# Summing the last gathered tile's value rows on VectorE, and taking the last dense column tile by tile, in a one-core encoder layer

## The chip, the cores and the metric

The kernel runs on one core of a Trainium2 chip. The time is device time in microseconds (us) of one launch. A core has TensorE (PE, with its weight loads as PEld), VectorE (DVE), ScalarE (ACT), GpSimd (POOL) and SyncE (SP), each with an instruction queue of its own that it works off in order, and 16 DMA engines that serve all queues.

## The reference

One encoder layer on 1024 tokens of width 1024: a projection, two token mixers, a merge, a layer norm, and then a layer of product-key experts (PEER) and a second layer norm. The change touches only the experts and the last norm:

```python
def _peer(x, w_q, sub_keys, u_table, v_table):
...
        q = (xb @ w_q).reshape(t, PEER_HEADS, 2, PEER_HALF)
...
        idx = jnp.take_along_axis(cand_i.reshape(t, PEER_HEADS, K * K), best_pos, axis=-1)
        gate = jax.nn.softmax(best_s, axis=-1).astype(xb.dtype)
        h = jax.nn.gelu(jnp.einsum('thkd,td->thk', u_table[idx], xb), approximate=False)
        return jnp.einsum('thk,thkd->td', gate * h, v_table[idx])
...
        x = _layer_norm(DN_ALPHA * x + _peer(x, peer_w_q[l], peer_sub_keys[l], peer_u[l], peer_v[l]),
                        ln2_g[l], ln2_b[l])
```

For each token 8 heads x 16 = 128 experts are selected out of 16384. Each expert has one key row in `u_table` and one value row in `v_table`, 1024 float32 each. The token's output is the sum over its 128 slots of gate x gelu(key row . x) x value row.

## The kernel before, in words

The 1024 tokens are 8 tiles of 128. Tiles 3, 4, 5 (`DENSE`) are computed densely, over all 16384 experts, on TensorE. Tiles 0, 1, 2, 6, 7 (`GATHERED`) gather only the rows that they selected.

**The dense loop.** `dense_block` runs over 128 columns j of 128 experts each. `hidden(j, m)` multiplies the key rows of a column with the hidden states of all three tiles into the PSUM tile `b` (24 products in two halves m). `csplit(j)` applies gelu on ScalarE, multiplies with the gates on VectorE (tile `C`), and splits the result into a high and a low part (`ch`, `cl`). `values(j, m)` multiplies that with one half of the column's value rows (`vh`, `vl`) into the six accumulators `po` (tiles `v`, 18 products a column). All products are done as three products of split operands; `usplit` and `vsplit` make these from the raw rows `uraw` and `vraw`: a cast on ScalarE and a subtraction on VectorE for one half and on GpSimd for the other. The raw rows, 512 KB for keys and 512 KB for values a column, are loaded through SP's queue, two and three columns ahead. Stage and place of everything else are told by the column.

**The gathered tiles.** For each slot k, `experts_in` has GpSimd issue an indirect DMA that fetches the key row of each of the 128 tokens (L1461, 512 KB, into the places `g` or `C` of `keys`), and VectorE reduces it against x into one column of `hh` (L1467). When a tile's 128 slots are done, `hh` goes through gelu and the gate and is stored to `cijd`. Then `Rows` takes over: `prepare` loads it and turns it on TensorE; `gather` has GpSimd issue indirect DMAs for value rows (L1763, 512 KB, into `vr` or `C`), where token and slot are arranged such that TensorE sums them with narrow products into the PSUM tile `pg`: 4 products for a pair of rows, each shown as 2 instructions in the trace, 16 for the two pairs that are done in one go. The sum is stored to `yd`, and `finals` loads it again, adds alpha x, normalizes and stores the tile.

**What sets the order.** PE, DVE and POOL issue in the order in which the code is written. `Background` objects put the gathered work between the products: each product of t us gives `rate` x t us of credit to `g.V` (`Rows`, rate `RATEV`) and to `g.B` (`experts_in`, rate `RATEB`), and a step with a cost is taken while there is credit. In the dense loop the rates before were 0.46 for `g.B` and 0.52 for `g.V`, and 1.25 for `g.V` once all keys were done. So tile 7's values came after its keys: its keys ended at column 103, and its value products filled columns 105 to 125.

**The end.** `finals` is stepped twice a column from column 44. For tile 7 and then for the dense tiles the norm ran after the loop on VectorE (`add` L1829, statistics L1266, `scale` L1277 and L1278).

Of the kernel before, what the change touches and what calls it, by code (L numbers as in the profile page):

```python
# [10 lines left out]
F32 = mybir.dt.float32  # L11
# [4 lines left out]
AF = mybir.ActivationFunctionType  # L16
OP = mybir.AluOpType
# [9 lines left out]
TKI = 1  # L27
RATEP = (1, 1, 0.9)

RATEB = (2.1, 0.46)  # L30
RATEV = (4.2, 0.52, 1.25)
SEL = (1, 2, 3)
DENSE = (3, 4, 5)
GATHERED = (0, 1, 2, 6, 7)
LATE = (4, 5, 6)

RING = 7
# [24 lines left out]
ALPHA = 2.0 ** 0.25  # L62
# [232 lines left out]
class Weights:  # L295
# [965 lines left out]
def layer_norm(g, mt, z):  # L1261

    dve, act = g.dve, g.act
    st = mt.tile([128, 2, 6], F32, name="st", bufs=3)
    for i in range(2):
        dve.bn_stats(st[:, i, :], z[:, i * 512:(i + 1) * 512])  # L1266
    yield
    mv = mt.tile([128, 2], F32, name="mv", bufs=3)
    dve.bn_aggr(mv, st)
    rs = mt.tile([128, 1], F32, name="rs", bufs=3)  # L1270
    act.activation(rs, mv[:, 1:2], AF.Sqrt, bias=g.eps[:, 1:2])
    yield
    dve.reciprocal(rs, rs)
    yield

    def scale(z, gb):
        dve.scalar_tensor_tensor(z, z, mv[:, 0:1], gb[0], op0=OP.subtract, op1=OP.mult)  # L1277
        dve.scalar_tensor_tensor(z, z, rs, gb[1], op0=OP.mult, op1=OP.add)  # L1278

    yield scale  # L1280
# [166 lines left out]
def experts_in(g, tile_):  # L1447

    dve, act, pool, sp, A, P = g.dve, g.act, g.pool, g.sp, g.A, g.gp
    idx = P.tile([128, 128], I32, name="eidx", bufs=1)  # L1450
    sp.dma_start(idx, g.seld[tile_])
    xt = P.tile([128, D], F32, name="ext")
    sp.dma_start(xt, g.x1d[tile_])
    hh = P.tile([128, 128], F32, name="hh", bufs=1)
    keys, n = g.keys, 0
    yield 1.0
    yield 1.0
    for k in range(128):
        while n < 128 and len(keys.free) > 1:
            keys.alive[n] = place = keys.take()  # L1460
            pool.indirect_dma_start(out=place, out_offset=None, in_=A["u"], in_offset=bass.IndirectOffsetOnAxis(ap=idx[:, n:n + 1], axis=0))  # L1461
            n += 1
# [4 lines left out]
        dve.tensor_tensor_reduce(out=gg, in0=gg, in1=xt, scale=1.0, scalar=0.0, op0=OP.mult, op1=OP.add, accum_out=hh[:, k:k + 1])  # L1467
# [12 lines left out]
def parts(C, i, a, b):  # L1480
# [4 lines left out]
def dense_block(g, C):  # L1485


    tc, nc, A, ident = g.tc, g.nc, g.A, g.ident
    dve, act, pool, sp, pe = g.dve, g.act, g.pool, g.sp, g.pe
    tiles = DENSE  # L1490
    nt = len(tiles)
    n = nt * 128
# [62 lines left out]
    with tc.tile_pool(name="bp", bufs=BLEAD + 1) as bp, tc.tile_pool(name="cj", bufs=2) as cj:  # L1555
        ab, pb = {}, {}
        for k in range(-BLEAD - 4, n4 + 1):
# [35 lines left out]
    u_hl, v_hl, c_hl, phs = {}, {}, {}, {}  # L1593
    po = [[g.psV.tile([128, 512], F32, name=f"v{i}{m}") for m in range(2)] for i in range(nt)]
# [92 lines left out]
    fin, old = iter(()), [p for j in range(LOOP, HALF - 7, 8) for i in range(nt) for p in parts(C, i, j, j + 8)]  # L1687
    g.rows.pairs = True
    for j in range(128):
        hidden(j + 1, 0)  # L1690
        usplit(2 * j + 4)
        hidden(j + 1, 1)
        usplit(2 * j + 5)
        csplit(j + 1)
        values(j, 0)
        vsplit(2 * j + 2)
        next(fin, None)
        values(j, 1)
# [118 lines left out]
def finals(g, tiles, po, places):  # L1817


    A, dve, act, sp = g.A, g.dve, g.act, g.sp  # L1820
    gb = places[0:2]
    for m in range(2):
        sp.dma_start(gb[m], A["ln"][2 + m:3 + m, :].to_broadcast([128, D]))
    zd = places[4:7]

    def add(z, y):
        for m in range(2):
            zm = z[:, m * 512:(m + 1) * 512]
            dve.scalar_tensor_tensor(zm, zm, ALPHA, y[m], op0=OP.mult, op1=OP.add)  # L1829

    z, y = places[2:4]
    for t in GATHERED:
        sp.dma_start(z, g.x1d[t])
        if t == GATHERED[-1]:
            while f"g{t}" not in g.B.done:
                yield
            for t_, z_ in zip(tiles, zd):
                sp.dma_start(z_, g.x1d[t_])
# [86 lines left out]
```

## Time and profile before

| | us |
|---|---|
| median of 3 runs | 3575.67 (3569.68 to 3590.42) |
| the profiled execution, its own time | 3567.98 |
| its span, first to last instruction | 3566.2 |
| dense loop, from the first product into `b` to the last product into `v` | 2195.0 to 3543.7 |

| engine | busy us | share of the span |
|---|---|---|
| PE | 3168.3 | 89% |
| DVE | 2252.5 | 63% |
| POOL | 2051.0 | 58% |
| ACT | 1161.9 | 33% |

The shares are means over stages with different limits. The dense loop is the last 38% of the span and is read by itself below. In the views, a group row ends with busy time, the mean of one instruction in ns, and the idle time of the engine just before instructions of the group with what ended it; a row of the table of stretches gives busy time per engine, the granted clock of TensorE, the busy share of the DMA engines and GB/s.

### The profile page before, as it was taken

The numbers are of one execution on the slowest core, as the hardware profiler recorded it, in microseconds if no ns is written. First come the engines' busy times: TensorE is split into PE (matmuls) and PEld (weight loads), VectorE is DVE, ScalarE is ACT, GpSimd is POOL, SyncE is SP. The second block draws the span as 40 slices with busy tenths as digits, with TensorE's granted clock in tenths as the row PEclk, the third lists the DMA queues.
The fourth block names the chain that finished last, engine by engine and source line by source line (L and its number), as shares of the span: only waits on it lengthen the run. The fifth ranks groups of instructions, "written<-read, shape, count | busy, mean of one in ns | idle before, by whom it ended". The sixth has DMA issues, their size and how long they took to land. (4 is left out here: it accounts for less than half of the span.)

```text
span 3566.2 us, 55635 instructions
## 1 busy us (share of the span) xinstructions
PE 3168.3 (89%) x20656; PEld 2312.2 (65%) x20656; DVE 2252.5 (63%) x5115; ACT 1161.9 (33%) x2448; POOL 2051.0 (58%) x1682
## 2 busy tenths in 40 slices
PE   7899999999997887889677677999999999999997
PEld 5577777875565665567433323877777777776665
DVE  3244423358887997886589755777666767773324
ACT  3443222323431121101244433334333333333332
POOL 2032115315555565653365566888887788886773
PEclk9999999999998788899778899999999999999998
DMA  8373357878897788999799999999999999999994
GB/s 282 112 255 110 105 190 250 306 272 313 287 348 290 272 302 307 350 358 383 278 392 351 354 361 379 369 353 362 386 398 368 394 394 399 397 396 341 389 390 188
DMA packets 369809, 1134.72 MB, mean 318 GB/s; under 512 B 49792, under 2 KB 88448, under 8 KB 367744
## 3 DMA queue, kind: packets, MB, share of 16 engines
q0 software_dynamic: 184320, 671.17, 49.5%
q1 hardware_dynamic: 168496, 430.82, 33.3%
q10 hardware_dynamic: 16720, 29.17, 2.2%
q8 instruction: 162, 2.65, 0.3%
q14 instruction: 111, 0.91, 0.1%
HBM read 997.25 MB, written 133.76 MB: 317 GB/s over the span
## 5 line engine op out<-in xcount | busy, mean ns | idle before, releaser
L1461 POOL DMA_INDIRECT g<-u,eidx x566 | 688.9, 1217 | 520.6 <-DVE hh L1467 193.9
L1467 DVE CUSTOM_DVE_ANT_0 g<-g,ext 128x1024 f32<-128x1024 f32 x566 | 727.9, 1296 | 84.2 <-DMA g<-u,eidx 78.2
L1763 POOL DMA_INDIRECT vr<-v,ve x434 | 454.9, 1048 | 212.0 <-issue 107.2
L292 POOL TENSOR_TENSOR wl<-wraw,wh 128x1024 fp32r<-128x1024 f32 x63 | 152.9, 2427 | 434.3 <-ACT wh L291 335.2
L274 PE MATMUL pg<-vr,win 128*32 128x512 f32 x1736 | 312.9, 643 | 65.6 <-DMA vr<-v,ve 57.9
L274 PE MATMUL b<-xh,uh 128*128 128x384 f32 x1024 | 349.8, 342 | 14.0 <-DVE C L1648 12.6
L274 PE MATMUL b<-xh,ul 128*128 128x384 f32 x1024 | 351.0, 343 | 6.2 <-POOL ul L292 4.3
L274 PE MATMUL b<-xl,uh 128*128 128x384 f32 x1024 | 348.7, 341 | 0.0
L274 PE MATMUL v<-vl,ch 128*128 128x512 f32 x768 | 305.0, 397 | 11.5 <-POOL vl L292 11.4
L274 PE MATMUL v<-vh,ch 128*128 128x512 f32 x768 | 302.5, 394 | 0.0
L274 PE MATMUL v<-vh,cl 128*128 128x512 f32 x768 | 300.8, 392 | 0.0
L274 PE MATMUL pj<-xh,wh 128*128 128x512 f32 x624 | 286.0, 458 | 13.6 <-ACT xh L291 6.6
L291 ACT CAST uh<-uraw 128x512 fp32r<-128x512 f32 x256 | 158.3, 620 | 362.6 <-PE b L274 254.7
L274 PE MATMUL pj<-xl,wh 128*128 128x512 f32 x624 | 260.0, 417 | 2.7 <-DVE xl L292 2.4
L274 PE MATMUL pj<-xh,wl 128*128 128x512 f32 x624 | 259.0, 415 | 0.2 <-issue 0.2
L1763 POOL DMA_INDIRECT C<-v,ve x206 | 212.0, 1029 | 81.4 <-issue 49.0
L292 DVE TENSOR_TENSOR vl<-vraw,vh 128x512 fp32r<-128x512 f32 x128 | 140.8, 1100 | 173.9 <-ACT vh L291 113.0
L291 ACT CAST vh<-vraw 128x512 fp32r<-128x512 f32 x256 | 158.3, 620 | 244.1 <-PE v L274 183.9
L274 PEld LDWEIGHTS v<-ab 128*128 128x128 f32 x768 | 112.5, 217 | 175.6 <-issue 112.9
L292 POOL TENSOR_TENSOR ul<-uraw,uh 128x512 fp32r<-128x512 f32 x128 | 171.6, 1340 | 89.2 <-ACT uh L291 73.6
L274 PEld LDWEIGHTS b<-xh,uh 128*128 128x128 f32 x1024 | 193.5, 189 | 34.5 <-DVE C L1648 14.8
L274 PEld LDWEIGHTS b<-xh,ul 128*128 128x128 f32 x1024 | 193.5, 189 | 32.8 <-issue 24.7
(360 smaller groups left out, 6603.9 us busy)
## 6 DMA issues: line engine op xcount, KB each, us to landing
uraw<-ut SPq DMA_DIRECT2D x128, 512.0 KB
vraw<-vt SPq DMA_DIRECT2D x128, 512.0 KB
wraw<-w SPq DMA_DIRECT2D x72, 512.0 KB
wh<-whd SPq DMA_DIRECT2D x72, 512.0 KB
wl<-whd SPq DMA_DIRECT2D x72, 512.0 KB
whd<-wh SPq DMA_DIRECT2D x71, 512.0 KB
whd<-wl SPq DMA_DIRECT2D x71, 512.0 KB
cd<-S SPq DMA_DIRECT2D x12, 1344.0 KB
```

The costliest lines, as they stand in the source:

```text
L274: g.pe.matmul(o, l, r, start=start, stop=stop_)
L291: g.act.copy(hi, src)
L292: (lo_eng or g.dve).tensor_sub(lo, src, hi.bitcast(F32))
L1461: pool.indirect_dma_start(out=place, out_offset=None, in_=A["u"], in_offset=bass.IndirectOffsetOnAxis(ap=idx[:, n:n + 1], axis=0))
L1467: dve.tensor_tensor_reduce(out=gg, in0=gg, in1=xt, scale=1.0, scalar=0.0, op0=OP.mult, op1=OP.add, accum_out=hh[:, k:k + 1])
L1763: g.pool.indirect_dma_start(out=place, out_offset=None, in_=g.A["v"], in_offset=bass.IndirectOffsetOnAxis(ap=self.meta[i][1][:, t:t + 1], ...
```

## The change

- `GATHERED` loses tile 7 (`LAST`), so `Rows` has four tiles instead of five. `experts_in` of tile 7 goes on after its 128 key rows with its 128 value rows: the same index column and the same ring of places, an indirect DMA on GpSimd for each, and one `scalar_tensor_tensor` of 128x1024 on VectorE that adds value row x `hh` to a tile `z`, which starts as alpha x. The gathering runs over the border between keys and values without a stop (`ahead`). The turning, the narrow products, and the store and load of `cijd` and `yd` are gone for tile 7.
- The rates in the dense loop become 0.58 for `g.B`, 0.6 from the point where tile 7's keys are selected, and 0.45 for `g.V` throughout.
- The last column's values products are issued tile by tile (both halves of tile 3's accumulators, then tile 4's, then tile 5's) instead of half by half.
- Tile 7's norm is made within the loop. The norms of the dense tiles are made tile by tile; the scaling of the second one goes to ScalarE (x rs - mean x rs) and GpSimd (times the gain, plus the bias), with its store on ScalarE's queue.

The diff, without the lines that only rename:

```diff
-RATEB = (2.1, 0.46)
-RATEV = (4.2, 0.52, 1.25)
+RATEB = (2.1, 0.58, 0.6)
+RATEV = (4.2, 0.45)
-GATHERED = (0, 1, 2, 6, 7)
+GATHERED = (0, 1, 2, 6)
+LAST = 7
...
+    ends = 256 if tile_ == LAST else 128
+    def ahead():
+        nonlocal n
+        while n < ends and len(keys.free) > 1:
+            keys.alive[n] = place = keys.take()
+            pool.indirect_dma_start(out=place, out_offset=None, in_=A["uv"[n // 128]], in_offset=bass.IndirectOffsetOnAxis(ap=idx[:, n % 128:n % 128 + 1], axis=0))
+            n += 1
...
+    g.last = z = g.rows.places.take()
+    sp.dma_start(z, g.x1d[tile_])
+    ahead()
+    yield 3.0
+    yield 3.0
     dve.tensor_mul(hh, hh, gate)
+    dve.tensor_scalar(z, z, ALPHA, None, op0=OP.mult)
+    for k in range(128):
+        ahead()
+        gg = keys.alive.pop(128 + k)
+        dve.scalar_tensor_tensor(z, gg, hh[:, k:k + 1], z, op0=OP.mult, op1=OP.add)
+        keys.give(gg)
+        yield 1.46
...
     def values(j, m):
         ch, cl = c_hl[j]
-        vh, vl = v_hl.pop(2 * j + m)
+        if j == 127 and m == 0:
+            return
         for i in range(nt):
             s = slice(i * 128, (i + 1) * 128)
-            mm3(g, po[i][m], ch[:, s], cl[:, s], vh, vl, j == 0, j == 127)
+            for q in (m,) if j < 127 else range(2):
+                mm3(g, po[i][q], ch[:, s], cl[:, s], *v_hl[2 * j + q], j == 0, j == 127)
+        v_hl.pop(2 * j + m)
...
-        if f"g{GATHERED[-1]}" in g.B.done:
-            g.V.rate = RATEV[2]
+        if f"v{GATHERED[-1]}" in g.V.done:
+            next(fin, None)
+            next(fin, None)
+        if f"k{LAST}" in g.B.done:
+            g.B.rate = RATEB[2]
...
+    ln = layer_norm(g, g.pp, g.last)
+    for _ in range(3):
+        next(ln)
+        yield
+    next(ln)(g.last, gb)
+    sp.dma_start(A["out"][LAST * 128:(LAST + 1) * 128, :], g.last)
     while not g.over:
         yield
     lns = []
     for i, z in enumerate(zd):
         add(z, po[i])
         lns.append(layer_norm(g, g.pp, z))
-    for _ in range(3):
-        for ln in lns:
-            next(ln)
-    for t, z, ln in zip(tiles, zd, lns):
-        next(ln)(z, gb)
-        sp.dma_start(A["out"][t * 128:(t + 1) * 128, :], z)
+        next(lns[i])
+        next(lns[i])
+        if i == 1:
+            next(lns[0])
+            next(lns[1])
+            mv, rs = next(lns[1]).__defaults__
+            dve.scalar_tensor_tensor(mv[:, 0:1], mv[:, 0:1], -1.0, rs, op0=OP.mult, op1=OP.mult)
+            act.activation(z, z, AF.Identity, scale=rs, bias=mv[:, 0:1])
+            g.pool.tensor_mul(z, z, gb[0])
+            g.pool.tensor_add(z, z, gb[1])
+            act.dma_start(A["out"][tiles[1] * 128:tiles[1] * 128 + 128, :], z)
+    next(lns[2])
+    for i in (0, 2):
+        next(lns[i])(zd[i], gb)
+        sp.dma_start(A["out"][tiles[i] * 128:(tiles[i] + 1) * 128, :], zd[i])
```

How the order of instructions changes, at three places.

GpSimd's queue around column 95 of the dense loop. Before: `u,eidx` are key rows for VectorE, `v,ve` value rows for TensorE, `ul` and `vl` the subtractions of the dense splits.

```order
L292 TENSOR_TENSOR vl<-vraw,vh 128x512
L1461 DMA C<-u,eidx 128x1024
L292 TENSOR_TENSOR ul<-uraw,uh 128x512
L1461 DMA C<-u,eidx 128x1024
L1763 DMA vr_14133<-v,ve 128x1024
L1763 DMA C<-v,ve 128x1024
L1763 DMA vr_14134<-v,ve 128x1024
L1763 DMA C<-v,ve 128x1024
L292 TENSOR_TENSOR vl<-vraw,vh 128x512
L1461 DMA g_70<-u,eidx 128x1024
L1461 DMA g_71<-u,eidx 128x1024
```

The same queue near the same column in the changed kernel, where `v,eidx` are tile 7's value rows for VectorE:

```order
L293 TENSOR_TENSOR vl<-vraw,vh 128x512
L1465 DMA g_72<-v,eidx 128x1024
L1465 DMA C<-v,eidx 128x1024
L293 TENSOR_TENSOR ul<-uraw,uh 128x512
L1465 DMA C<-v,eidx 128x1024
L293 TENSOR_TENSOR vl<-vraw,vh 128x512
L1465 DMA C<-v,eidx 128x1024
L1465 DMA g_68<-v,eidx 128x1024
L1793 DMA C<-v,ve 128x1024 x3
L1793 DMA vr_14134<-v,ve 128x1024
```

Between two subtractions there stand about as many gathers as before, but more of them are for VectorE. Counted over columns 26 to 122: before 179 for VectorE and 328 for TensorE, after 295 (167 key rows, 128 value rows) and 224; over columns 3 to 25: before 45 and 60, after 57 and 54.

VectorE's queue at the same place, one column, before (`ISA` with `ext` is the key row's reduction, `hh 128x1` its result's read):

```order
L1648 TENSOR_TENSOR C<-b,C 128x3x4x32
L292 TENSOR_TENSOR cl<-C,ch 128x384
L1467 ISA g_69,hh<-g_69,ext 128x1024
L1467 ISA hh 128x1
L292 TENSOR_TENSOR vl<-vraw,vh 128x512
L1467 ISA C,hh<-C,ext 128x1024
L1467 ISA hh 128x1
L292 TENSOR_TENSOR ul<-uraw,uh 128x512
```

and after:

```order
L1672 TENSOR_TENSOR C<-b,C 128x3x4x32
L293 TENSOR_TENSOR cl<-C,ch 128x384
L1499 SCALAR_TENSOR_TENSOR C<-g_71,hh,C 128x1024
L1499 SCALAR_TENSOR_TENSOR C<-g_72,hh,C 128x1024
L293 TENSOR_TENSOR vl<-vraw,vh 128x512
L293 TENSOR_TENSOR ul<-uraw,uh 128x512
L1499 SCALAR_TENSOR_TENSOR C<-C,hh 128x1024
```

The reductions of key rows end at column 80 instead of 103, and the value sums stand from column 82 to 122, three or four in a column.

VectorE's last instructions, before: first the six additions of the dense accumulators (`v_17411` to `v_17416` are the two halves of tile 3's, tile 4's and tile 5's), then all statistics.

```order
L1829 SCALAR_TENSOR_TENSOR C<-C,v_17411 128x512
L1829 SCALAR_TENSOR_TENSOR C<-C,v_17412 128x512
L1829 SCALAR_TENSOR_TENSOR C<-C,v_17413 128x512
L1829 SCALAR_TENSOR_TENSOR C<-C,v_17414 128x512
L1829 SCALAR_TENSOR_TENSOR C<-C,v_17415 128x512
L1829 SCALAR_TENSOR_TENSOR C<-C,v_17416 128x512
L1266 BN_STATS st<-C 128x6 x6
L1269 BN_AGGR mv<-st 128x2 x3
```

and after, where the first tile's statistics stand ahead of the second tile's additions:

```order
L1859 SCALAR_TENSOR_TENSOR C<-C,v_17411 128x512
L1859 SCALAR_TENSOR_TENSOR C<-C,v_17412 128x512
L1267 BN_STATS st<-C 128x6 x2
L1270 BN_AGGR mv<-st 128x2
L1859 SCALAR_TENSOR_TENSOR C<-C,v_17413 128x512
L1859 SCALAR_TENSOR_TENSOR C<-C,v_17414 128x512
L1267 BN_STATS st<-C 128x6 x2
L1270 BN_AGGR mv<-st 128x2
L1274 RECIPROCAL rs<-rs 128x1 x2
L1903 SCALAR_TENSOR_TENSOR mv<-mv,rs 128x1
L1859 SCALAR_TENSOR_TENSOR C<-C,v_17415 128x512
```

Tile 7's statistics and scaling, which stood ahead of the first fence's rows, have gone into the loop's last columns.

More of the change, by code (lines that the diff above doesn't have):

```diff
@@ L1274, in layer_norm, with scale @@
     yield
-    def scale(z, gb):
+    def scale(z, gb, mv=mv, rs=rs):
         dve.scalar_tensor_tensor(z, z, mv[:, 0:1], gb[0], op0=OP.subtract, op1=OP.mult)
@@ L1457, in experts_in @@
     yield 1.0
+    ends = 256 if tile_ == LAST else 128
[5 more added lines that the diff above has]
+            n += 1
     for k in range(128):
[L1459 to L1462, printed above, removed]
+        ahead()
         if k == 0:
@@ L1471, in experts_in @@
         sp.dma_start(g.dbg["hh"][tile_ * 128:(tile_ + 1) * 128, :], hh)
-    gate = idx.bitcast(F32)
+    gate = g.tk.tile([128, 128], F32, name="t1") if tile_ == LAST else idx.bitcast(F32)
     sp.dma_start(gate, g.gated[tile_])
     act.activation(hh, hh, AF.Gelu)
-    dve.tensor_mul(hh, hh, gate)
-    act.dma_start(g.cijd[tile_][:, 0, :], hh)
-    yield 0.1
+    if tile_ != LAST:
+        dve.tensor_mul(hh, hh, gate)
+        act.dma_start(g.cijd[tile_][:, 0, :], hh)
+        yield 0.1
+        return
+    while not g.rows.places.room(1):
+        yield 1.0
+    g.last = z = g.rows.places.take()
[3 more added lines that the diff above has]
+    yield 3.0
+    dve.tensor_mul(hh, hh, gate)
+    dve.tensor_scalar(z, z, ALPHA, None, op0=OP.mult)
+    for k in range(128):
+        ahead()
+        gg = keys.alive.pop(128 + k)
+        dve.scalar_tensor_tensor(z, gg, hh[:, k:k + 1], z, op0=OP.mult, op1=OP.add)
+        keys.give(gg)
+        yield 1.46
 def parts(C, i, a, b):
@@ L1667, in values @@
         ch, cl = c_hl[j]
-        vh, vl = v_hl.pop(2 * j + m)
+        if j == 127 and m == 0:
+            return
         for i in range(nt):
             s = slice(i * 128, (i + 1) * 128)
-            mm3(g, po[i][m], ch[:, s], cl[:, s], vh, vl, j == 0, j == 127)
+            for q in (m,) if j < 127 else range(2):
+                mm3(g, po[i][q], ch[:, s], cl[:, s], *v_hl[2 * j + q], j == 0, j == 127)
+        v_hl.pop(2 * j + m)
         if m:
@@ L1711, in dense_block @@
             fin = finals(g, tiles, po, old[-4:] + old[0:nt])
-    assert f"v{GATHERED[-1]}" in g.V.done
+    assert f"v{GATHERED[-1]}" in g.V.done and f"g{LAST}" in g.B.done
     g.over = True
@@ L1833, in finals @@
         sp.dma_start(z, g.x1d[t])
[L1834 to L1838, printed above, removed]
         while f"v{t}" not in g.V.done:
@@ L1855, in finals @@
         yield
+    while f"g{LAST}" not in g.B.done:
+        yield
+    for t, z in zip(tiles, zd):
+        sp.dma_start(z, g.x1d[t])
+    ln = layer_norm(g, g.pp, g.last)
+    for _ in range(3):
+        next(ln)
+        yield
+    next(ln)(g.last, gb)
+    sp.dma_start(A["out"][LAST * 128:(LAST + 1) * 128, :], g.last)
     while not g.over:
```

## The prediction

> **What bounds the kernel now.** I read the page first, for the shares of the whole span, then stretches of the dense loop, then the chain that ended last, then the groups of the stretch that the change touches, and last GpSimd's and VectorE's own rows.
>
> ```profile
> span 3566.2 us, 55635 instructions
> PE 3168.3 (89%) x20656; PEld 2312.2 (65%) x20656; DVE 2252.5 (63%) x5115; ACT 1161.9 (33%) x2448; POOL 2051.0 (58%) x1682
> ```
>
> By the page PE leads and GpSimd has 42% to spare. That mean hides the stage in question:
>
> ```profile
> core 0: us, PE busy (x) PEld busy (x) DVE busy (x) ACT busy (x) POOL busy (x), PEclk, DMA share, GB/s
> 2195.00:2462.00 267.00, 257.71 (x1364) 203.93 (x1365) 185.34 (x354) 98.11 (x198) 211.96 (x172) 0.98 0.96 358
> 2462.00:3490.00 1028.00, 997.17 (x5395) 767.75 (x5394) 608.63 (x802) 370.95 (x773) 828.22 (x705) 0.99 1.01 386
> 3490.00:3544.00 54.00, 53.68 (x291) 41.97 (x289) 16.23 (x27) 19.13 (x36) 20.95 (x19) 1.00 0.48 173
> 3544.00:3566.00 22.00, 0.00 (x0) 0.00 (x0) 17.82 (x27) 0.67 (x3) 0.00 (x0) 0.55 0.24 96
> ```
>
> These are columns 0 to 25, 26 to 122, 123 to 127, and the end. In the long stretch PE is busy 97%, the DMA engines 1.01 (their packets overlap, so they are full) and GpSimd 81% without its issue gaps. Three resources are near their limits at once. The chain tells how PE's columns are made up:
>
> ```profile
> 3073.86 4.24 PE b L274 x24
> 3078.11 4.17 PE v L274 x18
> ...
> 3083.33 1.85 PE pg L274 x16
> ...
> 3088.51 4.12 PE v L274 x18
> ```
>
> A column is 4.24 + 4.12 = 8.36 us of dense products. Two pairs of gathered value rows cost 1.85 us, one pair 0.925. Now the groups of the long stretch:
>
> ```profile
> L1763 POOL DMA_INDIRECT vr<-v,ve x197 | 204.6, 1039 | 55.6 <-issue 49.8 <-DMA g<-u,eidx 0.9 <-PE pg L274 0.9
> L1763 POOL DMA_INDIRECT C<-v,ve x137 | 143.5, 1048 | 39.7 <-issue 33.5 <-DVE ve L1751 2.2 <-PE b L274 0.9
> L1461 POOL DMA_INDIRECT g<-u,eidx x110 | 136.2, 1238 | 24.3 <-issue 16.7 <-DVE hh L1467 2.4 <-DVE cl L292 1.2
> L292 POOL TENSOR_TENSOR vl<-vraw,vh 128x512 fp32r<-128x512 f32 x97 | 133.7, 1378 | 13.2 <-ACT vh L291 12.0
> L292 POOL TENSOR_TENSOR ul<-uraw,uh 128x512 fp32r<-128x512 f32 x97 | 127.9, 1318 | 49.4 <-ACT uh L291 38.1 <-issue 9.8
> L274 PE MATMUL pg<-vr,win 128*32 128x512 f32 x776 | 126.4, 602 | 0.5 <-DMA vr<-v,ve 0.5
> L274 PE MATMUL pg<-C,win 128*32 128x512 f32 x536 | 95.7, 615 | 7.2 <-DMA C<-v,ve 7.2
> L1461 POOL DMA_INDIRECT C<-u,eidx x67 | 84.0, 1254 | 17.8 <-issue 10.7 <-DMA eidx<-seld 2.8 <-DVE hh L1467 1.5
> L1648 DVE TENSOR_TENSOR C<-b,C 128x384 f32<-128x384 f32 x97 | 53.8, 555 | 113.1 <-ACT b L1647 97.0 <-ACT uh L291 10.1 <-issue 5.8
> ```
>
> L1648 stands once in a column, so these are 97 columns. PE: 97 x 8.36 = 811, and (776 + 536) / 8 = 164 pairs x 0.925 = 152, together 963 of 1028 us; 65 us are stalls. GpSimd's price of a gather is its duration with the issue gap ahead of it, which no other work fills: for VectorE (136.2 + 24.3 + 84.0 + 17.8 - 2.8) / 177 = 1.47 us, for TensorE (204.6 + 55.6 + 143.5 + 39.7) / 334 = 1.33. The two subtractions cost 133.7 + 127.9 us, with gaps that aren't waits 2.73 a column. Sum 260 + 443 + 265 = 968, that is 94% of the stretch. So GpSimd isn't the idle engine that the page shows, but one of three that are full.
>
> **Why gathers for VectorE are dearer.**
>
> ```profile
> 3111.81 1.42 POOL L292 TENSOR_TENSOR vl<-vraw,vh 128x512 fp32r<-128x512 f32 x1
> 3113.38 1.76 POOL L1461 DMA_INDIRECT g<-u,eidx  x1
> 3115.45 0.94 POOL L1763 DMA_INDIRECT vr<-v,ve  x1 [0.30 <-issue]
> 3116.69 0.94 POOL L1763 DMA_INDIRECT C<-v,ve  x1 [0.30 <-issue]
> ...
> 3120.41 1.81 POOL L1461 DMA_INDIRECT C<-u,eidx  x1 [0.31 <-issue]
> ...
> 3112.02 2.29 DVE L1467 CUSTOM_DVE_ANT_0 C<-C,ext 128x1024 f32<-128x1024 f32 x1
> ```
>
> An unhindered gather takes 0.94 + 0.30 = 1.24 us. The one at 3113.38 ends at 3115.14, 0.83 after VectorE's reduction (3114.31) lets go; that reduction itself takes 2.29 because GpSimd's subtraction (to 3113.23) held it up. The two engines lock each other out for part of an instruction. [...]
>
> **The change, part by part.**
>
> *Columns 0 to 25: 0.* Over columns 3 to 25 the key gathers go from 45 to 57 and TensorE's from 60 to 54: PE gives back 3 pairs, 2.8 us, GpSimd gets 12 x 1.47 - 6 x 1.33 = 9.7 us more, and it was busy 212 of 267 there, before gaps. I take 0, bounds -3 and +10.
>
> *Columns 26 to 122: -15.* PE loses 164 - 112 = 52 pairs, 48 us. If PE alone were the limit the stretch would shrink by that and by stalls, to between 915 and 980. But bytes and gathers stay: they only move from one consumer to the other. GpSimd: 295 x 1.47 + 224 x 1.33 + 97 x 2.73 = 434 + 298 + 265 = 997 us. At the price of the densest part of the stretch,
>
> ```profile
> L1461 POOL DMA_INDIRECT g<-u,eidx x55 | 73.7, 1340 | 11.9 <-issue 6.8 <-DVE hh L1467 1.5 <-DVE cl L292 1.2
> L1461 POOL DMA_INDIRECT C<-u,eidx x35 | 44.5, 1270 | 7.6 <-issue 5.3 <-DVE hh L1467 1.2 <-DVE cl L292 0.3
> ...
> 2854.00:3262.00 408.00, 403.19 (x2173) 320.79 (x2172) 281.18 (x359) 148.30 (x302) 342.34 (x281) 1.00 1.02 393
> ```
>
> (137.7 / 90 = 1.53), it is 1014. DMA: 1028 us x 386 GB/s = 397 MB now; 519 gathers instead of 511 in the trace make it 401 MB; at the 393 GB/s of the densest part, with its share of 1.02, that takes 1020 us. Two independent limits thus stand at 997 to 1020 where PE needs 915. I take 1013, near the upper ones, because GpSimd was never without some idle time: 1028 to 1013 is -15. The bounds are 980 (below) and 1056 (rival A). The same engines then show another picture: PE idle some 10%, waiting for `ul` and `vl` behind gathers in GpSimd's queue. The stall at the passage from tile 7's keys to its values goes (the 7.2 us of the row `pg<-C,win`, part of the 65). VectorE gets 116 more rows of about 1.4 us in this stretch, 162 us on 609 of 1028, so 75%; its splits and `C` come later behind a sum of 1.2 us, which PE's next products cover (L1648 is wanted after the 4.12 us of `v`). Where this cover goes, PE stalls by the rest of the sum, at most 1.2 us a column. SP's queue has the same row loads; the store and load of `yd` for tile 7 and the turning of its `cijd` are gone, which costs nothing now at a DMA share of 0.48 in the last columns. ScalarE loses the small copies for 64 pairs; it is busy 36% and gates nothing.
>
> *Columns 123 to 127: -5.* Before, 8 pairs of tile 7 stand there, after 2 of tile 6: -5.5 us. In the last column taking tile 4's and 5's products later means that the second half of tile 3 needs the last split after 0.69 us instead of 2.06, while that split takes 1.3 us (0.63 on ScalarE, 0.69 on VectorE, rows below): +0.7. Tile 7's norm and two switches of ScalarE's function stand here too; they lie beside 4.24 us of `b`, and I take 0, at worst +2.
>
> *The end: -5.*
>
> ```profile
> 3539.50 0.63 ACT vh L291
> 3540.15 0.69 DVE vl L292
> 3540.85 1.20 DVE C L1829 x2
> ...
> 3546.52 3.59 DVE C L1829 x6
> 3550.11 3.57 DVE st L1266 x6
> ...
> 3560.93 1.28 DVE C L1278
> ...
> L292 POOL TENSOR_TENSOR wl<-wraw,wh 128x1024 fp32r<-128x1024 f32 x63 | 152.9, 2427 | 434.3 <-ACT wh L291 335.2 <-PE s L274 42.7 <-PE po L274 26.4
> ```
>
> Before, tile 7's norm holds VectorE until 3546.52, 2.8 us past the last product (3543.7), and everything ends at 3562.2, 18.5 us past it. After, tile 3 is complete 12 x 0.229 = 2.7 us before the last product, and VectorE has 3.6 + 3.6 of additions and statistics, about 1.4 of small ones and waits, and 4 scalings of 1.25, not 6: 13.6 us, to end 10.9 past the last product, -7.6. Against it: GpSimd's two 128x1024 steps take 2.43 each and, as above, lock VectorE's scalings out for up to 4.9 us. Bounds -7.6 and -2.7; I take -5, in the middle.
>
> **Sum:** 0 - 15 - 5 - 5 = -25 on the profiled execution's 3567.98: 3543. The median of the three runs lies 7.7 above that execution, so as a median 3551.
>
> **The rivals.**
>
> *A, slower: lockout on GpSimd.* The dear rows above cost 1.76 and 1.81 with 0.31, 2.1 us; now about a quarter of VectorE's gathers are like that ((1.47 - 1.24) / 0.86). If half are, the price is 1.67, the stretch 295 x 1.67 + 563 = 1056, +28, and the sum +18: 3586, as a median 3594. For it: VectorE will be busier by a quarter. Against: the price rises only from 1.47 to 1.53 in the densest part, where VectorE is busy 281 of 408. The change turns slower overall from a price of about 1.61.
>
> *B, PE stays the limit.* If issue gaps and DMA are more elastic than they look, the stretch falls to the 401 MB at the best rate that 40 us slices show (409 GB/s, an estimate from the next rows), 980 us, -48: 3510, as a median 3518.
>
> ```profile
> 2620.00:2660.00 40.00, 40.00 (x220) 31.84 (x220) 25.79 (x37) 14.81 (x31) 33.89 (x31) 1.00 1.03 409
> ...
> 2900.00:2940.00 40.00, 39.24 (x214) 30.62 (x213) 27.91 (x35) 13.92 (x29) 34.84 (x27) 1.00 1.04 395
> ```
>
> At 1.03 to 1.04 these slices span 395 to 409, which speaks against 409 for a thousand us. [...]
>
> *C, no change: the DMA rate stays.* At the stretch's mean of 386 GB/s the 401 MB take 1039, +11, and the sum is about 0: 3569, as a median 3577. For it: the loads of dense rows already land late behind gathers. Against: part of the mean are pauses that go.
>
> **How the numbers follow.** Forecast 0.52, A 0.15, B 0.12, C 0.21. A measurement of this kernel tells about 0.5%, 18 us, from no change. The forecast's own range is 3533 to 3567; of its 0.52, 0.42 lie below -18. Faster: 0.42 + 0.12 = 0.54; slower: 0.15; same: 0.31. The range 3512 to 3592 reaches to B and to A and leaves out less than 2 in 10.
>
> **What would show it.** Right: in the loop's stretch PE busy falls to about 90%, GpSimd with its gaps is at 97% or more, DMA share 1.02 at 390 to 398 GB/s, a gather for VectorE costs 1.45 to 1.55, stalls of PE end on `vl`, `ul` or late raw rows; after the last product 15 to 20 us remain instead of 22.5. Wrong: a price above 1.6, VectorE's rows ending PE's waits, or a rate of 405 GB/s and more.

## The result: 0.7% slower, and the profile after

The changed kernel takes 3609.73 us (median of 9 runs), the kernel before 3581.93 (median of 9); the ratio is 1.0071, 95% interval 1.0045 to 1.0097. One of the changed kernel's runs, at a granted clock of 0.688 where the others had 0.92 to 0.93, took 5042.85 us, and one of e6 below took 4861.22 at 0.599; the ratios leave both out. The forecast was 25 us less; it is about 25 us more, outside the range of 3512 to 3592.

The head of the page of the profiled execution, for comparison with the two lines shown of before:

```profile
span 3607.7 us, 54845 instructions
...
PE 3133.1 (87%) x20141; PEld 2318.2 (64%) x20141; DVE 2437.6 (68%) x5239; ACT 1151.0 (32%) x2383; POOL 2129.5 (59%) x1684
```

PE has 35 us less to do and the kernel is slower: PE is not what paces it. The same stretches as before, cut at the same columns (ahead of the loop, 0 to 25, 26 to 122, 123 to 127, the end):

```profile
core 0: us, PE busy (x) PEld busy (x) DVE busy (x) ACT busy (x) POOL busy (x), PEclk, DMA share, GB/s
0.00:2205.70 2205.70, 1860.31 (x13611) 1296.60 (x13611) 1424.79 (x3910) 672.32 (x1440) 990.06 (x788) 0.90 0.79 286
2205.70:2482.00 276.30, 255.70 (x1330) 201.46 (x1331) 216.27 (x391) 98.85 (x197) 225.56 (x175) 0.97 0.94 350
2482.00:3542.00 1060.00, 968.92 (x4961) 778.99 (x4960) 758.42 (x883) 354.31 (x707) 896.71 (x711) 0.97 0.99 376
3542.00:3590.00 48.00, 47.77 (x243) 41.18 (x242) 25.23 (x40) 23.46 (x38) 11.62 (x9) 1.00 0.29 98
3590.00:3607.00 17.00, 0.43 (x2) 0.01 (x1) 12.87 (x18) 2.02 (x4) 5.54 (x2) 0.62 0.23 93
```

| columns | before | after | difference | forecast |
|---|---|---|---|---|
| ahead of the loop (same program) | 2195.0 | 2205.7 | +10.7 | 0 |
| 0 to 25 | 266.8 | 276.5 | +9.7 | 0 (-3 to +10) |
| 26 to 122 | 1027.7 | 1059.5 | +31.8 | -15 (-48 to +28) |
| 123 to 127 | 54.2 | 48.8 | -5.4 | -5 |
| the end | 22.5 | 17.3 | -5.2 | -5 |

The first row is no effect of the change: in the profiled runs of e1 to e4 below, on one chip and with the same program up to there, the loop begins anywhere from 2162 to 2184 us. Without it 31 us are left, which fits the ratio. The loss is in the long stretch. Its groups, GpSimd's rows, VectorE's sums and the two PE rows with idle time:

```profile
L275 PE MATMUL b<-xh,ul 128*128 128x384 f32 x776 | 272.5, 351 | 51.6 <-POOL ul L293 51.5
L275 PE MATMUL v<-vl,ch 128*128 128x512 f32 x583 | 239.4, 411 | 35.6 <-POOL vl L293 35.6
L1793 POOL DMA_INDIRECT vr<-v,ve x138 | 164.3, 1191 | 40.2 <-issue 36.0 <-PE b L275 1.1 <-DMA C<-v,eidx 0.9
L293 POOL TENSOR_TENSOR vl<-vraw,vh 128x512 fp32r<-128x512 f32 x98 | 134.7, 1374 | 6.0 <-ACT vh L292 4.7
L293 POOL TENSOR_TENSOR ul<-uraw,uh 128x512 fp32r<-128x512 f32 x97 | 131.4, 1355 | 19.0 <-ACT uh L292 17.3
L1465 POOL DMA_INDIRECT g<-u,eidx x102 | 129.3, 1268 | 23.9 <-issue 19.4 <-DVE cl L293 0.6 <-DVE hh L1474 0.6
L1499 DVE SCALAR_TENSOR_TENSOR C<-g,hh,C 128x1024 f32<-128x1024 f32 x80 | 125.7, 1571 | 0.5
L1793 POOL DMA_INDIRECT C<-v,ve x86 | 102.5, 1192 | 25.3 <-issue 22.0 <-PE v L275 0.9 <-DMA C<-u,eidx 0.6
L1465 POOL DMA_INDIRECT g<-v,eidx x80 | 101.7, 1271 | 18.4 <-issue 14.8 <-DVE C L1499 0.6 <-DMA g<-v,eidx 0.6
L1499 DVE SCALAR_TENSOR_TENSOR C<-C,hh 128x1024 f32<-128x1024 f32 x48 | 77.5, 1615 | 0.4
L1465 POOL DMA_INDIRECT C<-u,eidx x62 | 74.4, 1200 | 18.8 <-issue 10.8 <-DVE C L1672 5.6 <-DVE cl L293 0.6
L1465 POOL DMA_INDIRECT C<-v,eidx x48 | 60.1, 1252 | 11.5 <-issue 8.6 <-DVE C L1672 0.9 <-DVE C L1499 0.6
```

PE waits 51.5 + 35.6 us for GpSimd's `ul` and `vl`. GpSimd has hardly an idle moment: gathers for VectorE (129.3 + 23.9 + 74.4 + 18.8 + 101.7 + 18.4 + 60.1 + 11.5) / 292 = 1.50 us each, 438 us; for TensorE (164.3 + 40.2 + 102.5 + 25.3) / 224 = 1.48, 332 us; subtractions 269 with the gaps that aren't waits for ScalarE; 21 us of 1060 remain. TensorE's gathers cost 1.33 before. They are the same instructions, and the change doesn't touch them; here is what lengthens them, from the rows of GpSimd and then of VectorE in column 88:

```profile
3169.24 0.94 POOL L1793 DMA_INDIRECT vr<-v,ve  x1 [0.30 <-issue]
3170.48 1.88 POOL L1793 DMA_INDIRECT vr<-v,ve  x1 [0.30 <-issue]
3172.67 1.01 POOL L1793 DMA_INDIRECT vr<-v,ve  x1 [0.30 <-issue]
```

```profile
3170.27 2.60 DVE L1499 SCALAR_TENSOR_TENSOR C<-C,hh 128x1024 f32<-128x1024 f32 x2
```

Three gathers for TensorE in a row: the middle one starts 0.2 us after the first of two value sums of VectorE begins, and takes 1.88 instead of 0.94. That sum ends at 3171.55, the gather 0.81 us later. I counted this over all rows of columns 26 to 122: a gather is beside when a reduction of a key row, a value sum or a norm's step of VectorE overlaps it.

| | gathers beside | their mean | the others' mean | VectorE's such rows |
|---|---|---|---|---|
| before | 232 of 510 (45%) | 1.27 us | 0.98 us | 0.197 per us, 1.35 us each |
| after | 362 of 515 (70%) | 1.34 us | 0.96 us | 0.292 per us, 1.51 us each |

The shares are those of chance meetings: rows per us x (row + 0.94) is 0.197 x 2.29 = 0.45 before and 0.292 x 2.45 = 0.72 after.

The means hide a plain rule, which the traces of all runs show where a gather meets one instruction of VectorE and no other. When it starts inside a row of 128x1024 with two inputs in SBUF, with 0.1 us or more of that row left, it ends 0.81 to 0.83 us after the row's end (9 in 10 of 490 gathers), whoever it is for. When it starts ahead of the row, it takes 0.94 (258 gathers). So a gather that comes second waits for all that is left of VectorE's instruction, and one that comes first isn't held up.

### The profile page after: what moved, and what is told of

Read it like the earlier page. It is cut to its first block, busy times and chain, and to the rows that moved or that the text cites. A ratio compares the mean times of both kernels' runs of the same rounds, so it can differ in the third digit from the quotient of the medians.

```text
span 3607.7 us, 54845 instructions
## 1 busy us (share of the span) xinstructions
PE 3133.1 (87%) x20141; PEld 2318.2 (64%) x20141; DVE 2437.6 (68%) x5239; ACT 1151.0 (32%) x2383; POOL 2129.5 (59%) x1684
## 5 line engine op out<-in xcount | busy, mean ns | idle before, releaser
L1465 POOL DMA_INDIRECT g<-u,eidx x569 | 699.0, 1228 | 523.5 <-DVE hh L1474 186.7
L1474 DVE CUSTOM_DVE_ANT_0 g<-g,ext 128x1024 f32<-128x1024 f32 x569 | 751.9, 1330 | 78.4 <-DMA g<-u,eidx 76.3
L1793 POOL DMA_INDIRECT vr<-v,ve x359 | 404.1, 1126 | 187.2 <-issue 87.0
L293 POOL TENSOR_TENSOR wl<-wraw,wh 128x1024 fp32r<-128x1024 f32 x63 | 152.6, 2423 | 438.9 <-ACT wh L292 347.3
L275 PE MATMUL v<-vl,ch 128*128 128x512 f32 x768 | 313.8, 409 | 43.3 <-POOL vl L293 43.0
L275 PE MATMUL pg<-vr,win 128*32 128x512 f32 x1436 | 263.8, 644 | 70.2 <-DMA vr<-v,ve 61.9
L293 DVE TENSOR_TENSOR cl<-C,ch 128x384 fp32r<-128x384 f32 x128 | 119.9, 936 | 144.5 <-ACT ch L292 128.3
L1793 POOL DMA_INDIRECT C<-v,ve x153 | 168.8, 1103 | 73.2 <-issue 36.1
L275 PEld LDWEIGHTS v<-vl,ch 128*128 128x128 f32 x768 | 148.8, 194 | 95.4 <-POOL vl L293 58.1
```

The lines of the kernel that those rows point to most:

```text
L275: g.pe.matmul(o, l, r, start=start, stop=stop_)
L293: (lo_eng or g.dve).tensor_sub(lo, src, hi.bitcast(F32))
L1793: g.pool.indirect_dma_start(out=place, out_offset=None, in_=g.A["v"], in_offset=bass.IndirectOffsetOnAxis(ap=self.meta[i][1][:, t:t + 1], ...
```

## The experiments

Theory Q: GpSimd's queue, made longer by these meetings, is the limit of the changed kernel's long stretch. Rival D: the DMA rate is, and gathers are long because the DMA engines take no more (their share is 0.99). Rival V: VectorE comes late. The parts' times are cut at the first dense product of columns 0, 26, 82 and 123 of the profiled runs; ratios are to the kernel before, on the same chip. Each part is one execution's: e7 below, the same program as the changed kernel up to the last column, takes 276.6, 621.5 and 438.9 us, so a part repeats to 4 us or so.

| run | ratio, 95% interval | 0 to 25 | 26 to 81 | 82 to 122 |
|---|---|---|---|---|
| before | 1 | 266.8 | 570.4 | 457.3 |
| after | 1.0071 (1.0045 to 1.0097) | 276.5 | 618.0 | 441.4 |
| e1, `ul` on VectorE | 0.9934 (0.9910 to 0.9957) | 264.0 | 592.8 | 421.1 |
| e2, the same in before | 0.9977 (0.9955 to 0.9998) | 265.1 | 568.6 | 451.0 |
| e3, half value rows | 1.0064 (1.0043 to 1.0086) | 275.7 | 617.8 | 434.6 |
| e4, one-input value sums | 1.0028 (1.0009 to 1.0047) | 273.9 | 617.3 | 419.2 |
| e8, longer one-input sums | 1.0033 (1.0006 to 1.0060) | 275.8 | 615.9 | 428.2 |
| e9, one-input key reductions | 0.9969 (0.9943 to 0.9996) | 262.2 | 586.8 | 442.4 |
| e6, e1 and half value rows | 0.9897 (0.9863 to 0.9931) | 265.4 | 593.7 | 402.5 |
| e5, e1 with rates 0.58, 0.58, 0.44 | 0.9906 (0.9879 to 0.9933) | 265.8 | 585.9 | 406.8 |
| e10, e1 with 0.57, 0.6, 0.44 | 0.9935 (0.9912 to 0.9958) | 263.3 | 593.3 | 418.4 |
| e11, e1 with 0.57, 0.585, 0.45 | 0.9897 (0.9875 to 0.9920) | 260.0 | 594.7 | 413.3 |

**e1: work off GpSimd's queue, changed kernel.**

```diff
-UPOOL = (0, 1)
+UPOOL = (0, 0)
```

> The changed kernel with the subtractions that make `ul` on VectorE and not on GpSimd. Theory Q (GpSimd's in-order queue is the limit of columns 26 to 122, which take 1060 us): 97 x 1.36 = 131 us leave that queue, and the stretch falls by at least 40 us, to 930 to 1020 (whatever limit comes next), the kernel to 3480 to 3570. Theory D (the DMA rate is the limit, and GpSimd's gathers are long because the DMA takes no more): the stretch stays within 1045 to 1070 us and the kernel within 0.5% of the changed one; gathers only get dearer, from 1.49 to about 1.7 us. Theory V (VectorE is the limit): it gets 97 x 0.6 = 58 us more, the stretch grows by 20 us or more.

The long stretch falls by 46 us and the kernel becomes faster than both others: Q, and neither D nor V as the first limit. The ratio of 0.9934 is outside the noise, though small.

```profile
2184.30:2448.30 264.00, 252.93 (x1331) 203.01 (x1332) 196.01 (x418) 98.91 (x197) 187.90 (x149) 0.97 0.97 371
2448.30:3462.20 1013.90, 947.68 (x4959) 766.95 (x4958) 740.86 (x980) 346.98 (x706) 775.39 (x612) 0.98 1.02 393
```

With the queue relieved by 131 us the DMA engines move 393 GB/s where they moved 376. Columns 0 to 25 come back too (276.5 to 264.0): the 9.7 us lost there were the same queue's.

**e2: the same edit in the kernel before.**

> The kernel before, with the `ul` subtractions on VectorE and not on GpSimd, to see which limit it had (columns 26 to 122 took 1028 us, PE's own work 963). Theory Q: GpSimd loses 97 x 1.32 = 128 us, so PE is left as the limit and the stretch falls to 965 to 1000, the kernel by 30 to 60 us. Theory D: the stretch stays at 1015 to 1040. Theory V: it grows, because `ul` and `C` come later on VectorE.

```profile
2432.20:3451.80 1019.60, 992.95 (x5394) 769.74 (x5393) 580.88 (x899) 367.80 (x772) 709.20 (x606) 0.99 1.01 389
```

128 us taken off GpSimd bring 8 us of 1028: within the forecast of D (1015 to 1040), not Q's 965 to 1000. What limited the kernel before was not GpSimd's queue; the DMA rate (389 GB/s) and PE itself, busy 97%, are left, and no run parts these two. The change did not lengthen a queue that was the limit; it made it one.

**e3: half the bytes of the moved rows, changed kernel.**

```diff
-            pool.indirect_dma_start(out=place, out_offset=None, in_=A["uv"[n // 128]], ...)
+            f = 1 + n // 128
+            pool.indirect_dma_start(out=place[:, 0:D // f], out_offset=None,
+                in_=A["uv"[n // 128]].rearrange("r (a c) -> (r a) c", a=f), ...)
```

> The changed kernel, with the 128 gathers of tile 7's value rows fetching rows of 512 instead of 1024 elements (the other half of each row is left out; the number of instructions of every engine stays). The DMA engines have 128 x 256 KB = 33.6 MB less to move in columns 82 to 122, which take 441 us. Theory D: at 386 GB/s that is 87 us less, and the part falls to what PE needs, about 385 us, so by 45 to 60 us. Theory Q with lockout alone as the cause of dear gathers: no gather gets cheaper, the part stays at 430 to 445 us. Between them (gathers get cheaper because the DMA queue takes them faster): prices of 1.25 to 1.35 instead of 1.49, and the part falls by 20 to 45 us.

The row of columns 82 to 122, in this run and then in the changed kernel:

```profile
3061.70:3496.30 434.60, 405.83 (x2091) 327.15 (x2090) 329.52 (x291) 146.59 (x291) 367.00 (x292) 0.98 0.89 304
```

```profile
3100.20:3541.70 441.50, 407.77 (x2092) 328.33 (x2091) 319.67 (x291) 145.27 (x291) 370.27 (x293) 0.97 0.99 374
```

A fifth fewer bytes (132 against 165 MB, at 304 and 374 GB/s) and 7 us, where D asked for 45 to 60. D is out for the changed kernel, though its DMA share reads 0.99.

**e4 and e8: the value sums with one SBUF input.**

```diff
-        dve.scalar_tensor_tensor(z, gg, hh[:, k:k + 1], z, op0=OP.mult, op1=OP.add)
+        dve.tensor_reduce(hh[:, k:k + 1], gg, axis=AX.X, op=OP.add)
+        dve.tensor_reduce(hh[:, k:k + 1], gg[:, 0:512], axis=AX.X, op=OP.add)   # e8 alone
```

> The changed kernel, with each value row of tile 7 only summed over its elements into a column of `hh` (one SBUF input, about 1.1 us) instead of being multiplied and added to `z` (two inputs, 1.57 us): the weighted sum is left out, all DMAs stay. Theory Q with lockout by VectorE's two-input instructions as the cause of the dear gathers: prices in columns 82 to 122 fall from 1.49 to 1.25 to 1.35 us for VectorE's and TensorE's gathers, that is 215 gathers x 0.2 = 43 us, and the part falls from 441 us to 395 to 415. Theory D: prices and part stay (435 to 445 us), because the same bytes go. Theory V: the part falls by PE's waits for `C` only, 2 us.

> The changed kernel with each value row of tile 7 summed over its elements twice, once whole and once over its first half, instead of being multiplied and added to `z`: instructions with one SBUF input that together take longer (about 1.2 + 0.65 = 1.85 us) than the two-input sum (1.58 us); the weighted sum is left out. It parts two readings of the run with one short one-input sum, where gathers fell from 1.49 to 1.30 us. Lockout by two inputs: the price stays at 1.27 to 1.35 and columns 82 to 122 take 415 to 425 us, although VectorE is busier than in the changed kernel. Any busy VectorE slows GpSimd: the price rises to 1.45 or more and the part takes 435 us or more.

A gather's price falls from 1.49 us to 1.31 in e4, as forecast; columns 82 to 122 fall by 22 us, to 419, less than the forecast of 395 to 415. The row of this part in e4:

```profile
3053.10:3472.30 419.20, 399.90 (x2092) 326.35 (x2091) 280.35 (x291) 143.96 (x291) 324.65 (x292) 0.98 1.02 394
```

With the dear gathers gone the part runs at 394 GB/s, about the 393 at which e1 stops too: it has met the next limit (e6 below). e8 has VectorE busier than the changed kernel (358 us against 320 in this part); its rows of GpSimd there:

```profile
3055.60:3483.80 428.20, 399.33 (x2092) 323.88 (x2091) 358.06 (x420) 141.74 (x291) 315.13 (x292) 0.97 1.01 384
```

```profile
L1465 POOL DMA_INDIRECT g<-v,eidx x75 | 75.9, 1012 | 22.0 <-issue 8.2 <-DVE hh L1500 6.9 <-DVE hh L1499 3.4
...
L1794 POOL DMA_INDIRECT vr<-v,ve x56 | 54.2, 968 | 16.7 <-issue 13.3 <-PE b L275 1.2 <-DMA C<-v,eidx 0.8
L293 POOL TENSOR_TENSOR ul<-uraw,uh 128x512 fp32r<-128x512 f32 x41 | 53.9, 1314 | 44.3 <-ACT uh L292 43.8
L1465 POOL DMA_INDIRECT C<-v,eidx x46 | 46.3, 1005 | 13.9 <-issue 6.5 <-DVE hh L1500 3.9 <-DVE hh L1499 2.4
L1794 POOL DMA_INDIRECT C<-v,ve x32 | 31.5, 983 | 9.3 <-issue 7.9 <-PE b L275 0.6 <-DMA g<-v,eidx 0.3
```

Gathers take 0.97 to 1.01 us beside 1.9 us of one-input work for each row, where they took 1.16 to 1.28 beside sums of 1.58; the price is 1.29. So it isn't how long VectorE is busy that counts. The part takes 428, 3 more than forecast: with 44 us of waits for ScalarE's `uh`, the queue is no longer full.

These two runs change two things of VectorE's instruction at once: `tensor_reduce` has one SBUF input, and it writes one column where the sum writes a whole row. The traces of all runs part them, again where a gather meets one instruction alone. `C<-b,C` of 128x384 writes as much as `cl<-C,ch` of 128x384, but its input `b` lies in PSUM: 102 gathers that start inside it take 0.94 us, as do 66 that start inside a `tensor_reduce` of 1024 elements; 16 that start inside `cl<-C,ch` take 1.12 on average and end 0.83 after it. So it is the second SBUF input and not the write.

**e9: the key reductions of tiles 6 and 7 with one input, changed kernel.** This is where most was lost, columns 26 to 81.

```diff
+        if tile_ > 5:
+            dve.tensor_reduce(hh[:, k:k + 1], gg, axis=AX.X, op=OP.add)
+        else:
             dve.tensor_tensor_reduce(out=gg, in0=gg, in1=xt, ..., accum_out=hh[:, k:k + 1])
```

> The changed kernel, with the key rows of tiles 6 and 7 only summed over their elements (one SBUF input) instead of being multiplied with x (two inputs); the products with x are left out for these tiles, all DMAs and the value sums stay. Columns 26 to 81 lost most (570 us before, 618 after) and hold key rows almost alone. Lockout by two-input instructions: their 163 + 7 + 136 gathers fall from 1.48 to 1.24 to 1.30 us, which takes 55 to 70 us off GpSimd's queue; the part falls to where the DMA rate stops it (234 MB at 394 GB/s), 588 to 605 us, columns 82 to 122 stay at 435 to 445, and the kernel gets 20 to 40 us faster than the changed one: a ratio to the kernel before of 0.996 to 1.002. Rival, the larger number of gathers for VectorE in these columns makes the loss by itself: prices and the 618 us stay, ratio 1.006 to 1.008.

```profile
2461.00:3047.90 586.90, 549.87 (x2869) 445.54 (x2868) 396.47 (x422) 207.25 (x415) 460.26 (x417) 0.97 1.02 397
3047.90:3490.30 442.40, 405.99 (x2092) 325.76 (x2091) 316.16 (x292) 145.56 (x291) 370.67 (x292) 0.98 0.99 372
```

```profile
L1465 POOL DMA_INDIRECT g<-u,eidx x101 | 104.3, 1033 | 24.8 <-issue 16.6 <-DVE hh L1475 3.8 <-DVE cl L293 1.3
L1796 POOL DMA_INDIRECT vr<-v,ve x81 | 83.8, 1034 | 27.4 <-issue 21.3 <-PE b L275 3.0 <-PE pg L275 1.3
```

The part falls from 618 to 587, at 397 GB/s; the value columns stay at 442, and 0 to 25 (tile 6's keys) fall to 262. By these rows a gather costs 1.28 us for VectorE and 1.37 for TensorE (forecast 1.24 to 1.30), in the changed kernel's same columns 1.50 for both. So the key rows' reductions, set denser by the new rate (0.58 for 0.46), cost by meetings what the sums do: 31 us in 56 columns, as the sums cost 22 in 41.

**e6: is the DMA rate what is left in e1?** Both edits together.

> Two edits at once: `ul` on VectorE, and tile 7's value rows fetched half as wide (the other half of each row is left out). With `ul` on GpSimd half rows took 7 us from columns 82 to 122 (441 to 434), so bytes were not its limit. Theory: with 41 x 1.38 us taken off GpSimd's queue the DMA rate is what is left (421 us at 393 GB/s); then half rows now bring what they did not bring before, and the part falls to 390 to 405 us, PE's own work being 41 x 8.36 + 46 x 0.925 = 385. Rival: VectorE's lateness is what is left (PE waits 33 us for its `C` in the whole stretch); then the part stays at 412 to 421.

The row of columns 82 to 122 of e6, and of e1:

```profile
3030.10:3432.70 402.60, 394.30 (x2092) 321.79 (x2091) 317.57 (x332) 143.40 (x291) 320.61 (x251) 0.99 0.93 328
```

```profile
3041.00:3462.20 421.20, 398.61 (x2092) 321.87 (x2092) 318.35 (x334) 141.90 (x291) 322.25 (x251) 0.98 1.02 393
```

The same half rows that brought 7 us with `ul` on GpSimd bring 19 without: D is the next limit behind Q.

**e7: the end in its old order.**

```diff
-            for q in (m,) if j < 127 else range(2):
+            for q in (m,):
...
-        next(lns[i])
-        next(lns[i])
-        if i == 1:
...
+    for _ in range(3):
+        for ln in lns:
+            next(ln)
+    for t, z, ln in zip(tiles, zd, lns):
+        next(ln)(z, gb)
+        sp.dma_start(A["out"][t * 128:(t + 1) * 128, :], z)
```

> The changed kernel with the end as it was before the change: the last column half by half, all additions ahead of all statistics, and all three scalings on VectorE; tile 7's norm stays inside the loop. It splits the 5.2 us that the end became shorter (22.5 to 17.3 us after the last product) into the norm of tile 7, moved into the loop, and the new order. Theory of the prediction's working: from the end of tile 7's norm (2.8 us past the last product) 2.8 us come from that norm, so 19 to 20 us stand after the last product, and the order of tiles and engines gives the other 2 to 3. Rival: all comes from the norm's move, and 17 to 18 us stand there here too.

```profile
3505.10:3553.30 48.20, 48.19 (x245) 41.48 (x243) 24.33 (x38) 23.43 (x37) 11.78 (x10) 1.00 0.29 99
3553.30:3571.10 17.80, 0.00 (x0) 0.00 (x0) 13.48 (x21) 0.67 (x3) 0.00 (x0) 0.59 0.22 88
```

These are columns 123 to 127 and the end; e7 ran once, for its trace. 17.9 us stand after the last product against 17.3: the rival was right. Of the 5.2 us, 4.6 come from tile 7's norm having moved into the loop: the additions no longer stand behind it, and end 1.8 us past the last product in e7, 6.4 past it in the kernel before. The 0.6 of the new order are given back in the last columns, 48.2 us here and 48.8 in the changed kernel. Both parts together take 66.0 us in e7 and in the changed kernel, so the new order and the two other engines bring nothing.

**e5, e10, e11: a better kernel.** e1 leaves the DMA engines idle in the last columns (94 GB/s), so the gathers may reach further.

```diff
-UPOOL = (0, 1)
+UPOOL = (0, 0)
-RATEB = (2.1, 0.58, 0.6)
-RATEV = (4.2, 0.45)
+RATEB = (2.1, 0.57, 0.585)    # e11; e5: 0.58, 0.58; e10: 0.57, 0.6
+RATEV = (4.2, 0.45)           # e5 and e10: 0.44
```

> The changed kernel with `ul` on VectorE, and with the gathers spread further: rate 0.58 for `g.B` throughout and 0.44 for `g.V`, so that the last value rows are gathered at column 122 and 123 instead of 119 and 120. If the DMA rate is the limit that is left (393 GB/s in columns 26 to 122 against 94 GB/s in the last columns), 3 columns' worth of idle DMA time are used and the kernel loses 5 to 15 us against the one with `ul` on VectorE alone: a ratio to the kernel before of 0.989 to 0.992. If the limit is VectorE's lateness or GpSimd, the ratio stays at 0.993 or rises by the norm of tile 7, which then stands later, up to 0.996.

> The changed kernel with `ul` on VectorE and rates 0.57, 0.6 (`g.B`) and 0.44 (`g.V`): tile 7's value rows are gathered up to column 120 as in the first run with `ul` on VectorE, TensorE's value rows up to column 122 instead of 119. It is to keep what the run with rates 0.58 and 0.44 gained in columns 26 to 122 (1014 to 993 us) without what that lost at the end (17.6 to 24.4 us, tile 7's norm after the loop). If the gathers' spread makes the gain: stretch 990 to 1005, end 17 to 18, ratio 0.987 to 0.991. If it was the later value rows of tile 7 alone: stretch 1008 to 1016, ratio 0.993.

> The changed kernel with `ul` on VectorE and rates 0.57, 0.585 (`g.B`) and 0.45 (`g.V`): TensorE's value rows end at column 119 as in the first run with `ul` on VectorE, tile 7's at column 123. If tile 6's late value rows were what made the end 7 us longer in the last run, it is 17 to 19 us here; and if the more even rate of `g.B` was what made columns 26 to 122 take 993 us, they take 990 to 1000: a ratio to the kernel before of 0.987 to 0.991. If neither, stretch 1010 to 1015 and end 24, ratio 0.993 to 0.995.

The long stretch, the last columns and the end of e11, and the end of e10:

```profile
2451.30:3459.20 1007.90, 946.71 (x4958) 768.64 (x4956) 722.58 (x973) 345.56 (x704) 769.38 (x611) 0.97 1.02 393
3459.20:3508.80 49.60, 48.86 (x244) 41.47 (x244) 40.80 (x54) 24.71 (x40) 11.81 (x7) 1.00 0.47 165
3508.80:3526.00 17.20, 0.00 (x1) 0.00 (x0) 12.44 (x17) 1.83 (x3) 5.54 (x2) 0.57 0.23 92
```

```profile
3528.30:3552.70 24.40, 0.00 (x0) 0.00 (x0) 18.68 (x28) 2.42 (x5) 5.54 (x2) 0.56 0.26 106
```

e5's ratio (0.9906) came as expected, its end of 24.4 us did not. e10's stretch (1011.7) and ratio fall on its second branch, that tile 7's later value rows alone made e5's stretch of 992.7. But e11, where these rows go to column 123 as in e5, takes 1007.9, so they alone don't make it; and the more even rate of `g.B`, by which e11 was to take 990 to 1000, doesn't either. Why e5's stretch is so short is open.

The end is clearer. e10, with tile 7's rows not later than in e1, has the same 24.4 as e5: it isn't tile 7's rows that delay the end but TensorE's, whose last gather stands in column 122 in both. Tile 6's norm then comes late, and tile 7's, behind it in `finals`, ends after the loop. In e11 TensorE's gathers end in column 120, as in e1, and the end is 17.3. e11 is 1.0% faster than before (0.9897, 0.9875 to 0.9920), and e5's interval overlaps it.

## Why the prediction was wrong

*What bounds the kernel.* The three candidates were the right ones, but "one of three that are full" was too much for GpSimd at 94% of the stretch (95% with the 9.8 us of issue gap in the row of `ul`, which the 265 leaves out): e2 shows the kernel before at 386 to 389 GB/s whether GpSimd is relieved or not.

*Columns 26 to 122, -15.* Here it failed. The term was GpSimd's: 295 x 1.47 + 224 x 1.33 + 265 = 997, and 16 above it to the 1013 that was taken. Measured: gathers for VectorE 438 us (forecast 434), subtractions 269 (265), the rest 21 (16), and TensorE's gathers 332 instead of 298. These 34 of the 47 us are the step "224 x 1.33": a price read in a stretch with fewer two-input rows of VectorE was held constant for the one class of gathers that isn't moved, while the only price put in doubt was the other class's, and that stayed (1.50, forecast 1.45 to 1.55). The classes by consumer were the wrong ones. Before, TensorE's gathers were cheap because many of them stood in columns where VectorE had little to do (in columns 82 to 122, 25 of 180 met such a row); what makes a gather dear is a meeting, whoever it is for. Rows of before could have given the number: 45% of its gathers met one, and with 295 reductions and sums instead of 179 that share grows to some 70% (0.45 x 295 / 179 = 0.74).

*Rival A* named the mechanism and nearly the time (1056, measured 1060), but by a price of 1.67 on VectorE's gathers alone; its turn point of 1.61 was never reached and the kernel still turned slower. It had 0.15. The argument held against it, that the price rises only to 1.53 in the densest part, was read off the same class.

*Why gathers for VectorE are dearer* was read off a mean, 1.47 us, and that mean hides what a meeting costs: it mixes gathers that met nothing, gathers that came first, and gathers that came second and waited for all that was left of VectorE's row. The dear gather at 3113.38 that the prediction shows is one of the last kind: it ends 0.83 us after the reduction, as 9 in 10 such gathers of all runs end 0.81 to 0.83 us after the row. So each such meeting costs the rest of a row, and not each gather a whole one: 1.34 us on average beside in the changed kernel, 0.96 for the others. Gathers inside an instruction of VectorE with one SBUF input took no longer than unhindered ones: 0.94 us inside `tensor_reduce` (66 gathers) and inside `C<-b,C` (102).

*DMA, 1020.* A fair bound, for another kernel: e1, whose queue is relieved, takes 1013.9 us at 393 GB/s. The forecast of 390 to 398 GB/s for this one failed (376); the highest rate of a part in the rows above is 397 GB/s (columns 26 to 81 of e9). *Rival B* is out (PE 91% busy, waiting for `ul` and `vl`, as forecast), and *C*'s 386 GB/s is what before had, not after.

*VectorE's lateness* at no cost was right: PE waited 3.8 us for it in the stretch, although a value sum took 1.57 to 1.62 us there and not the 1.2 of the working.

*Columns 0 to 25, 0.* Its bound of +10 was the value: the same prices (+9.7, given back in e1 and e9).

*Columns 123 to 127, -5:* -5.4, for the stated reasons: the +0.7 for the last column's split is there (13.4 us for that column against 12.8 before, and 12.9 in e7 in the old order), and the pairs that are gone gave 6.1. *The end, -5:* -5.2, but that it lies so near is luck in part. The norm's move gave 4.6, where the working had 2.8; the new order gave 0.6, since VectorE's last rows in the chain show what GpSimd's two steps, 2.34 and 3.20 us from 3594.52 to 3600.14, take back:

```profile
3596.32 1.63 DVE C L1278
3597.98 3.24 DVE C L1279
3601.22 1.21 DVE C L1278
```

The first two rows take 1.63 + 3.24 instead of 1.21 + 1.28, 2.4 us more, of the up to 4.9 that were feared. With what it adds in the last column the new order is worth nothing.

*What would show it wrong* listed a price above 1.6, VectorE's rows in PE's waits, and 405 GB/s. None came. The list watched only the terms that were already in doubt.

## What to carry to other kernels

Where two engines slow each other, cost every instruction of both in that stretch again, the unmoved ones first, by how often they will meet (rows per us x the sum of the two durations: 0.72 for the changed kernel, where 70% were counted) and by how much of the other's instruction is left when the second one starts. Here an engine at 94% with its gaps was not yet the limit; halving one resource's load at a time shows which one is, and which is next. A change that takes work off one engine and puts none on the limit may still make a new limit by contention, and then pays only after that queue is relieved: here with one subtraction a column moved away, from 0.7% slower to 0.7% faster, and to 1.0% faster with the rates of e11.

## What the runs showed of the hardware

The DMA engines' share of time said little near 1 here: it read 0.99 at 374 GB/s, where a fifth fewer bytes gained 7 us of 441, and 1.02 at 393, where they gained 19 of 421. A gather that started inside a VectorE instruction with two SBUF inputs ended 0.81 to 0.83 us after that instruction (9 in 10 of 490 gathers in rows of 128x1024, all runs); one that started ahead of it (258 gathers), or inside an instruction with one SBUF input (168), took 0.94. Beside such rows gathers took 1.27 us on average before and 1.34 after (VectorE's 1.33 and 1.38, TensorE's 1.21 and 1.28), and half as wide rows cost no less (1.29 beside, 0.96 alone in columns 82 to 122 of e3, where GpSimd was busy 367.0 us for 292 instructions, against 370.3 for 293 in the changed kernel).
